# A hybrid RWKV-7 and attention layer: the RWKV batch stage for both token halves in one call, with V centred as it is turned

## The chip, the cores and the metric

The kernel runs on one core of a Trainium2 chip. The metric is the device time of one execution in microseconds; for each kernel the median of several runs is given, and one further execution is profiled. TensorE, VectorE, ScalarE and GpSimd are called PE, DVE, ACT and POOL in the rows, and SP is the engine that issues most DMAs; PEld are weight loads of TensorE.

## What is computed

One decoder layer on 1024 tokens of width 1024, all in float32: a norm and one wide projection; two parallel branches, RWKV-7 time mixing and dilated attention, each behind a sigmoid gate; a cross-attention to 256 memory rows; a squared-ReLU MLP; a last norm. The change lies in the RWKV branch, 16 heads of 64 channels:

```
for each token t and head:               # r, w, k, v, a, b have 64 channels
    sa    = state @ a_t                  # a = -kk, b = kk * a
    state = state * w_t + sa (x) b_t + v_t (x) k_t
    y_t   = state @ r_t
mean, var of y_t over the 64 channels
yn    = (y - mean) * rsqrt(var + eps) * gn_w + gn_b
out   = (yn + sum(r * k * r_k) * v) * g
```

v enters y linearly, channel by channel. So a v whose mean over the 64 channels of its head is taken off gives a y whose mean is zero; the bonus term sum(r k r_k) v needs v as it is.

## The kernel before

**Data.** Tokens are cut in two halves of 512, a half in 8 chunks of 64. Channels lie on the 128 partitions, two heads of 64 at a time: a pair p, eight pairs in all. The recurrence is computed in chunks: all that doesn't depend on the state is done for 8 chunks of a half as a batch of small matrix products, and then `scan` walks the chunks in order with one 64x64 state per head.

**Dense products.** `product` (L138) multiplies an 8 x 128 deep weight with a half of the activations. Weights and activations are split in a high and a low fp32r part, so each of the 8 steps is three matmuls of 128x128 by 512 columns (L143 to L145), and the generator yields after each three. `dense` (L328) does both halves; `proj` makes r, k and v of a pair with it, `gate` the gates.

**Stages of a pair.** `prep_a` makes decay and normed kk from two low-rank products; `psw` and `psa` get one 128-row matmul each with the high part of w2 and a2 and one 64-row matmul with the low part (L452 ff.). `prep_b` makes the tiles a, r, b, k and the products of them (`pa`, L528 ff.): per half two blocks of 8 fp32 matmuls of 64 rows, head 0 on the upper and head 1 on the lower half of the array's rows. VectorE masks them into A. `prep_d` turns V (`pvt`, four transposes) and b, k (`pb`), and multiplies the strictly lower part of A with V. `solve` and `solve_pe` invert a unit lower triangle, the first on VectorE, the second with fp32 matmuls on 32-row and 64-row tiles. `post` has per half a transpose and six batch products with the inverse: it makes the S tile, from which `scan` works. `gnorm` norms the result: `block_sum` sums over a head's 64 channels with a block-diagonal matrix of ones, once for the mean (`pm`) and once for the squares (`pvv`).

**Rows and columns of the array.** A batch product is `both` (L444):

```
ps = pms.tile([P, 8, CH], F32, tag="m", name=nm("po"))
for c in range(8):
    for h, hh in enumerate(heads()):
        mm(ps[hh, c, :], *fn(c, h, hh))
```

The head chooses the output partitions, so the column half of the array; `rows(half)` chooses the input partitions, so the row half. Half 0 works on rows 0 to 63 and half 1 on rows 64 to 127. An fp32 matmul is two instructions in the trace, so one call of `both` is 32. In two of the products (BK with UV, UV with A) all 128 rows are read.

**The order of the work.** `weave` (L151) merges generators: each has a number of steps and a stretch of a nominal 0 to 100, and the step that is due first goes next. The dictionary W (L761) has the due stretches: scan `s0`, `s1`; norm `g0`, `g1`; `b0` to `d1`, `so`, `sp`, `po`, `a0`, `a1` for the preparation of the next pair. `proj` of the pair after that and the gates fill in between. One call of `weave` is one iteration; there are nine, p = -1 to 7, the last without preparation. On top of this order the compiler's planner issues an instruction earlier when it expects that the one ahead isn't ready; `tc.issue_after` holds it to an order.

**PSUM.** Eight banks: two for dense products (`pacc`), three for all small products (`pms`), two for the scan's pz (`psc`), one for its y (`py`).

Of the kernel before, what the change touches and what calls it, by code (L numbers as in the profile page):

```python
# [17 lines left out]
P = 128  # L18
# [23 lines left out]
def hybrid_layer(ctx, tc, x, mem, norm_mix_g, w_in, shift_mu, w0, w2, a0, a2, g2, k_k, k_a, r_k, gn_w, gn_b,  # L42
# [230 lines left out]
    with tc.tile_pool(name="ra", bufs=1, side="right", reuse_waits="tile") as ra, \  # L273
# [3 lines left out]
            tc.tile_pool(name="pms", bufs=3, space=PSUM, reuse_waits="tile") as pms, \  # L277
            tc.tile_pool(name="psc", bufs=2, space=PSUM, reuse_waits="tile") as psc, \
# [29 lines left out]
        nc.vector.tensor_tensor(id2[:, 0, :], ident[:, 0:CH], ident[:, CH:P], op=ALU.add)  # L308
        WD = ra.tile([P, S], F32R, name="WD")
# [18 lines left out]
        def dense(src, evac, m=P):  # L328

            w = wload(src, NK, m, nc.gpsimd)  # L330
            for half in range(2):
                yield from product(w, acts(half), lambda ps: evac(half, ps[0:m, :]), m)

        def low_rank(blk):
# [28 lines left out]
            if blk == 0:  # L363
                evac(0, plr[0])
                yield from product(wlr, acts(1), lambda ps: evac(1, ps))
# [33 lines left out]
        def proj(p, cols="rkv"):  # L399
            if p not in st:  # L400
                st[p] = d = {"rkv": [{}, {}]}
                wa = [(rb if i else wrp[-1]).tile([P, 2, P], dt, tag=("wr", "wa1", "wa2")[i], name=nm("wa"), bufs=1 if i else None)
                      for i, dt in enumerate((F32, F32R, F32R))]
# [40 lines left out]
        def both(fn):  # L444

            ps = pms.tile([P, 8, CH], F32, tag="m", name=nm("po"))
            for c in range(8):
                for h, hh in enumerate(heads()):
                    mm(ps[hh, c, :], *fn(c, h, hh))
            return ps  # L450

        def prep_a(p, half):  # L452
# [3 lines left out]
            wah, wal = d["wa"]  # L456
# [5 lines left out]
            mm(psw, wal[0:64, 0, :], WD[0:64, hs], False, True)  # L462
            mm(psa, wal[64:128, 1, :], AD[64:128, hs], False, True)
# [32 lines left out]
        def prep_b(p, half):  # L496
# [24 lines left out]
            for q in range(2):  # L521
# [19 lines left out]
        def prep_d(p, half):  # L541
# [9 lines left out]
            for q in range(4):  # L551
                nc.tensor.transpose(pvt[:, q, :], v[:, q * P:(q + 1) * P], ident)
# [119 lines left out]
        def post(p, half):  # L672


            d = st[p]
            Am = d["Am"]
            ar, UV, BK, gC = [d[half][x] for x in ("ar", "UV", "BK", "gC")]
            m0 = half * 16
            us = rows(half)[0]
            if half == 0:  # L680
                d["S"] = rA.tile([P, 2, 4, 8, CH], F32, tag="A", name=nm("S"))
            St = d["S"][:, half]
            nc.gpsimd.tensor_tensor(St[:, 0], id2.broadcast_to([P, 8, CH]), gC.broadcast_to([P, 8, CH]), op=ALU.mult)

            pt = pms.tile([P, 4, P], F32, tag="m", name=nm("paT"))
            for q in range(4):
                nc.tensor.transpose(pt[:, q, :], d[half]["ara"][:, 0, 2 * q:2 * q + 2, :], ident)
            WT = r3.tile([P, 8, P], F32, tag="bk", name=nm("WT"), bufs=2)
            wtp = WT[us].rearrange("p (q e) f -> p q e f", e=2)
            nc.scalar.copy(wtp[:, :, 0, :], pt[0:64])  # L690
            nc.vector.tensor_copy(wtp[:, :, 1, :], pt[64:128])
            yield
            pu = both(lambda c, h, hh: (Am[us, m0 + 2 * c + h, 0:64], UV[us, c, hh]))
            for hh in heads():
                nc.scalar.copy(UV[us, :, hh], pu[hh])
            yield
            pw = both(lambda c, h, hh: (Am[us, m0 + 2 * c + h, 0:64], WT[us, c, hh]))

            Wm = Am[us, m0:m0 + 16, 0:64].rearrange("p (c h) t -> p c h t", h=2)
            for h, hh in enumerate(heads()):  # L700
                (nc.vector.tensor_copy if h else nc.scalar.copy)(Wm[:, :, h, :], pw[hh])
            yield
            ps = both(lambda c, h, hh: (Am[us, m0 + 2 * c + h, 0:64], BK[us, c, hh]))
            nc.vector.tensor_tensor(St[:, 0], St[:, 0], ps, op=ALU.add)
            yield
            ps = both(lambda c, h, hh: (BK[:, c, hh], UV[:, c, hh]))
            nc.scalar.copy(St[:, 2], ps)
            yield
            ps = both(lambda c, h, hh: (Am[us, m0 + 2 * c + h, 0:64], Am[us, m0 + 2 * c + h, 64:128]))
            nc.vector.tensor_tensor(St[:, 1], ar[:, :, 1, :], ps, op=ALU.add)  # L710
            yield
            ps = both(lambda c, h, hh: (UV[:, c, hh], Am[:, m0 + 2 * c + h, 64:128]))
            nc.scalar.copy(St[:, 3], ps)
            yield
# [21 lines left out]
        def gnorm(p, half):  # L736
# [7 lines left out]
            pm = pms.tile([P, H2], F32, tag="m", name=nm("pm"))  # L744
            block_sum(pm, y)
            yield
            nc.vector.scalar_tensor_tensor(y, pm, -1.0 / 64, y, op0=ALU.mult, op1=ALU.add)
# [14 lines left out]
                 d1=(28, 38), sp=(36, 54), c0=(40, 44), c1=(45, 49), po=(56, 82), a0=(62, 78), a1=(76, 94))  # L762
        W0 = dict(b0=(20, 29), b1=(28, 37), so=(37, 52), d0=(38, 45), d1=(44, 51), sp=(52, 66), c0=(50, 54), c1=(54, 58),
                  po=(68, 90), a0=(68, 82), a1=(80, 96))
# [4 lines left out]
        for p in range(-1, 8):  # L769
# [9 lines left out]
            if p < 6:  # L779
                cut = 42 if p >= 0 else 50  # L780
                sts.append((proj(p + 2, "krv"), 48, cut, 100))
# [4 lines left out]
            sts.append((chain(*DN), 16 * max(n, 1), 0, cut))  # L786
            if p >= 0:
                sts += [(scan(p, 0), 8, *W["s0"]), (scan(p, 1), 8, *W["s1"]),
                        (gnorm(p, 0), 6, *W["g0"]), (gnorm(p, 1), 6, *W["g1"])]
            if p < 7:  # L790
                for h in "01":
                    sts += [(prep_b(p + 1, int(h)), 5, *V["b" + h]), (prep_d(p + 1, int(h)), 4, *V["d" + h]),
                            (prep_c(p + 1, int(h)), 3, *V["c" + h])]
                sts += [(solve(p + 1), 22, *V["so"]), (solve_pe(p + 1), 10, *V["sp"]),
                        (chain(post(p + 1, 0), post(p + 1, 1)), 14, *V["po"])]
# [907 lines left out]
```

## Time and profile before

| | |
|---|---|
| median of 3 runs | 2513.06 us (2507.98 to 2517.85) |
| profiled execution | 2522.45 us |
| its span | 2520.7 us, mean granted TensorE clock 0.974 |
| RWKV stage in it | some 72 to 1020 us |
| busy over the span | TensorE 95%, VectorE 64%, ScalarE 42%, GpSimd 36% |
| matmul instructions | 18613 |

The span runs from the first to the last instruction. A matmul's length in the timeline has a modelled end and overlaps the next one, so what it costs on a busy TensorE is the time from its start to the start of the next.

### The profile page before, as it was taken

To read this page: it belongs to the slowest core of one execution; us is meant where nothing else is said; L and a number is where in the kernel's file an instruction comes from. 1 tells how busy PE (TensorE), PEld (TensorE's weight loads), DVE (VectorE), ACT (ScalarE), POOL (GpSimd) and SP (SyncE) were. 2 spreads that over 40 slices of the span, in tenths; PEclk is the share of its full clock that TensorE was granted. 3 is DMA by queue.
4 is the path that set the end of the run, shared out by engine and by line. 5 is a ranking of instruction groups with operands and counts; after the bars stand their busy time and mean duration, and the time that the engine had idled before them with its cause. 6 is when DMAs were issued, how large, how long until landed. Compare 5 with 4: busy or idle time off the path is not lost. (4 is left out here: it accounts for less than half of the span.)

```text
span 2520.7 us, 46875 instructions
## 1 busy us (share of the span) xinstructions
PE 2400.2 (95%) x18613; PEld 1886.7 (75%) x18613; DVE 1601.1 (64%) x2754; ACT 1060.0 (42%) x2048; POOL 918.0 (36%) x740
## 2 busy tenths in 40 slices
PE   6999999999999999999999999999979999899997
PEld 5787767777777777777767888788758888577775
DVE  6546675666656642224266565445799999887795
ACT  5434645445454443333344345444432222343344
POOL 4321222212222123211135533523665554556654
PEclk9999999999999999999979999999989999999998
DMA  4221111011111112321145554222234445654342
GB/s 168 54 65 28 36 37 33 29 31 36 37 33 32 39 44 82 83 60 43 47 133 161 162 161 144 82 59 84 71 117 152 152 145 163 192 159 122 109 139 75
DMA packets 301618, 226.72 MB, mean 90 GB/s; under 512 B 16229, under 2 KB 252375, under 8 KB 301399
## 3 DMA queue, kind: packets, MB, share of 16 engines
q1 hardware_dynamic: 301111, 223.20, 29.3%
q8 instruction: 146, 2.39, 0.4%
q10 hardware_dynamic: 288, 0.52, 0.1%
q14 instruction: 73, 0.60, 0.1%
HBM read 169.99 MB, written 53.67 MB: 89 GB/s over the span
## 5 line engine op out<-in xcount | busy, mean ns | idle before, releaser
L143 PE MATMUL acc<-ah,wh 128*128 128x512 f32 (+1 forms) x1600 | 666.7, 417 | 9.7 <-DVE h L1023 3.0
L112 POOL TENSOR_TENSOR wl<-wr,wh 128x512 fp32r<-128x512 f32 x248 | 333.5, 1347 | 820.7 <-ACT wh L110 798.1
L144 PE MATMUL acc<-al,wh 128*128 128x512 f32 (+1 forms) x1600 | 620.5, 388 | 2.8 <-POOL al L231 1.5
L145 PE MATMUL acc<-ah,wl 128*128 128x512 f32 (+1 forms) x1600 | 620.5, 388 | 0.0
L143 PEld LDWEIGHTS acc<-ah,wh 128*128 128x128 f32 x1600 | 303.5, 190 | 83.0 <-issue 7.0
L145 PEld LDWEIGHTS acc<-ah,wl 128*128 128x128 f32 x1600 | 302.8, 189 | 62.1
L144 PEld LDWEIGHTS acc<-al,wh 128*128 128x128 f32 x1600 | 305.2, 191 | 46.3 <-POOL al L231 3.3
L1394 PE MATMUL ms<-ah,wh 128*128 128x512 f32 x768 | 310.2, 404 | 17.2 <-DVE sg L1404 15.7
L1395 PE MATMUL ms<-al,wh 128*128 128x512 f32 x768 | 309.4, 403 | 17.2 <-DVE al L129 12.0
L1396 PE MATMUL ms<-ah,wl 128*128 128x512 f32 x768 | 307.5, 401 | 1.0 <-POOL wl L1357 1.0
L110 ACT CAST wh<-wr 128x512 fp32r<-128x512 f32 (+1 forms) x296 | 179.5, 607 | 289.4 <-PE acc L144 196.9
L1357 POOL TENSOR_TENSOR wl<-ws,wh 128x512 fp32r<-128x512 f32 x128 | 184.2, 1443 | 155.0 <-ACT wh L1356 148.6
L1395 PEld LDWEIGHTS ms<-al,wh 128*128 128x128 f32 x768 | 148.2, 193 | 56.1 <-DVE al L129 17.1
L1394 PEld LDWEIGHTS ms<-ah,wh 128*128 128x128 f32 x768 | 148.1, 193 | 54.7 <-ACT ah L128 8.4
L1357 POOL TENSOR_TENSOR wl<-sr,wh 128x512 fp32r<-128x512 f32 x96 | 142.8, 1488 | 122.2 <-ACT wh L1356 117.4
L1396 PEld LDWEIGHTS ms<-ah,wl 128*128 128x128 f32 x768 | 148.1, 193 | 35.4 <-POOL wl L1357 2.6
L1356 ACT CAST wh<-ws 128x512 fp32r<-128x512 f32 x128 | 79.3, 620 | 203.1 <-PE ms L1395 159.6
L1356 ACT CAST wh<-sr 128x512 fp32r<-128x512 f32 x96 | 59.2, 620 | 137.9 <-PE ms L1395 124.4
L912 DVE CUSTOM_DVE_ANT_0 sS<-pS,bias 128x128 f32<-128x128 f32 (+1 forms) x96 | 30.2, 349 | 114.8 <-PE pS L125 114.4
L129 DVE TENSOR_TENSOR al<-ur,ah 128x512 fp32r<-128x512 f32 x96 | 96.6, 1043 | 0.9 <-ACT ah L128 0.7
L128 ACT CAST ah<-ur 128x512 fp32r<-128x512 f32 x96 | 58.4, 619 | 64.0 <-DMA ur<-uscr 58.4
L917 ACT ACTIVATE sS<-sS,nm 128x128 f32<-128x128 f32 (+1 forms) x96 | 42.5, 443 | 76.6 <-DVE nm L915 72.1
(415 smaller groups left out, 4140.0 us busy)
## 6 DMA issues: line engine op xcount, KB each, us to landing
sr<-in_ffn_w_dram SPq DMA_DIRECT2D x134, 256.0 KB
wr<-in_w_in_dram SPq DMA_DIRECT2D x120, 256.0 KB
ur<-uscr SPq DMA_DIRECT2D x112, 256.0 KB
uscr<-sg SPq DMA_DIRECT2D x93, 256.0 KB
gtscr<-gt SPq DMA_DIRECT2D x32, 256.0 KB
g<-gtscr SPq DMA_DIRECT2D x32, 256.0 KB
wr<-in_p_rwkv_dram SPq DMA_DIRECT2D x32, 256.0 KB
wr<-in_w_out_dram SPq DMA_DIRECT2D x32, 256.0 KB
```

The lines of the kernel that those rows point to most:

```text
L110: nc.scalar.copy(h, raw)
L112: lo_eng.tensor_tensor(l, raw, h.bitcast(F32), op=ALU.subtract)
L128: nc.scalar.copy(hi, src)
L129: (lo_eng or nc.vector).tensor_tensor(lo, src, hi.bitcast(F32), op=ALU.subtract)
L143: mms.append(nc.tensor.matmul(ps, h, ah, start=(k == 0), stop=False))
L144: mms.append(nc.tensor.matmul(ps, h, al, start=False, stop=False))
L145: mms.append(nc.tensor.matmul(ps, l, ah, start=False, stop=(k == len(acts) - 1)))
L1356: nc.scalar.copy(h, raw)
L1357: nc.gpsimd.tensor_tensor(l, raw, h.bitcast(F32), op=ALU.subtract)
L1394: nc.tensor.matmul(ps, h[:, k, :], ah, start=(k == 0), stop=False)
L1395: nc.tensor.matmul(ps, h[:, k, :], al, start=False, stop=False)
L1396: nc.tensor.matmul(ps, l[:, k, :], ah, start=False, stop=(k == 3))
```

## The change

It does six things. (1) `four` takes the place of `both`: it computes the products of both halves in one call, alternating half 0 and half 1 for each chunk, with one PSUM tile for each half; `post` is one generator of 7 steps for both halves, and the batch product at the end of `prep_d` becomes a stage of its own, `prep_e`, due at 37 to 39. In `post` the product of BK and UV now stands ahead of that of A and BK. (2) V is turned by a product with `cen` (the identity less 1/64 within each head's block) and not by a transpose, so that it is centred; `gnorm` loses the sum `pm` and what used it. (3) The `pa` matmuls are chained one behind another by `issue_after`. (4) `product` has a step: in the RWKV stage it yields after six matmuls and not after three, and the numbers of steps are halved. (5) The low parts of w2 and a2 lie in a tile that is zero elsewhere, so that all four matmuls of `prep_a` use 128 rows. (6) `pms` has four banks, `psc` one.

```diff
-    def product(w, acts, evac, m=P, n=H2):
+    def product(w, acts, evac, m=P, n=H2, step=1):
...
-            if k < len(acts) - 1:
+            if k < len(acts) - 1 and k % step == step - 1:
                 yield
...
-            tc.tile_pool(name="pms", bufs=3, space=PSUM, reuse_waits="tile") as pms, \
-            tc.tile_pool(name="psc", bufs=2, space=PSUM, reuse_waits="tile") as psc, \
+            tc.tile_pool(name="pms", bufs=4, space=PSUM, reuse_waits="tile") as pms, \
+            tc.tile_pool(name="psc", bufs=1, space=PSUM, reuse_waits="tile") as psc, \
...
+        wal = ra.tile([P, 2, P], F32R, name="wal")
+        nc.gpsimd.memset(wal.bitcast(F32), 0.0)
+
+        cen = ra.tile([P, P], F32, name="cen")
+        nc.vector.scalar_tensor_tensor(cen, bones_r.bitcast(F32), -1.0 / 64, ident, op0=ALU.mult, op1=ALU.add)
...
-                yield from product(w, acts(half), lambda ps: evac(half, ps[0:m, :]), m)
+                yield from product(w, acts(half), lambda ps: evac(half, ps[0:m, :]), m, step=2)
...
-                nc.gpsimd.tensor_tensor(wa[2], wa[0], wa[1].bitcast(F32), op=ALU.subtract)
-                d["wa"] = wa[1:]
+                for j in range(2):
+                    js = slice(64 * j, 64 * j + 64)
+                    nc.gpsimd.tensor_tensor(wal[js, j, :], wa[0][js, j, :], wa[1][js, j, :].bitcast(F32), op=ALU.subtract)
+                d["wa"] = wa[1]
...
+        def four(fn):
+
+
+            ps = [pms.tile([P, 8, CH], F32, tag="m", name=nm("po")) for _ in range(2)]
             for c in range(8):
-                for h, hh in enumerate(heads()):
-                    mm(ps[hh, c, :], *fn(c, h, hh))
+                for half in range(2):
+                    for h, hh in enumerate(heads()):
+                        mm(ps[half][hh, c, :], *fn(half, c, h, hh))
             return ps
...
-            mm(psw, wal[0:64, 0, :], WD[0:64, hs], False, True)
-            mm(psa, wal[64:128, 1, :], AD[64:128, hs], False, True)
+            mm(psw, wal[:, 0, :], WD[:, hs], False, True)
+            mm(psa, wal[:, 1, :], AD[:, hs], False, True)
...
-                first = pa(0, 1)
-                with tc.issue_after(first.ins):
-                    pa(0, 0)
-                    for i in range(1, 4):
-                        for h in range(2):
-                            pa(i, h)
+                last = pa(0, 1)
+                for i in range(4):
+                    for h in range(2 if i else 1):
+                        with tc.issue_after(last.ins):
+                            last = pa(i, h)
...
-                nc.tensor.transpose(pvt[:, q, :], v[:, q * P:(q + 1) * P], ident)
+
+                mm(pvt[:, q, :], v[:, q * P:(q + 1) * P], cen)
...
-            ps = both(lambda c, h, hh: (d["Am"][vs, half * 16 + 2 * c + h, 0:64], UV[vs, c, hh]))
-            for hh in heads():
-                nc.scalar.copy(UV[us, :, hh], ps[hh])
+
+        def prep_e(p):
+            d = st[p]
+            UV = [d[half]["UV"] for half in range(2)]
+            ps = four(lambda half, c, h, hh: (d["Am"][rows(half)[1], half * 16 + 2 * c + h, 0:64],
+                                              UV[half][rows(half)[1], c, hh]))
+            for half in range(2):
+                for hh in heads():
+                    nc.scalar.copy(UV[half][rows(half)[0], :, hh], ps[half][hh])
             yield
...
-        def post(p, half):
+        def post(p):
...
+            pu = four(lambda f, c, h, hh: (am(f, c, h), UV[f][us(f), c, hh]))
+            for f in range(2):
+                for hh in heads():
+                    nc.scalar.copy(UV[f][us(f), :, hh], pu[f][hh])
+            yield
+            pw = four(lambda f, c, h, hh: (am(f, c, h), WT[f][us(f), c, hh]))
...
+            ps = four(lambda f, c, h, hh: (BK[f][:, c, hh], UV[f][:, c, hh]))
+            for f in range(2):
+                nc.scalar.copy(St[:, f, 2], ps[f])
+            yield
+            ps = four(lambda f, c, h, hh: (am(f, c, h), BK[f][us(f), c, hh]))
...
-            pm = pms.tile([P, H2], F32, tag="m", name=nm("pm"))
-            block_sum(pm, y)
-            yield
-            nc.vector.scalar_tensor_tensor(y, pm, -1.0 / 64, y, op0=ALU.mult, op1=ALU.add)
             nc.scalar.activation(q, y, AF.Square)
...
-                (chain(post(p + 1, 0), post(p + 1, 1)), 14, *V["po"])]
+                (prep_e(p + 1), 1, *V["e"]), (post(p + 1), 7, *V["po"])]
```

## Rows read from the trace of the kernel before

**Rows 1.** The page: engine shares (busy us, share of the span, instructions).

```profile
PE 2400.2 (95%) x18613; PEld 1886.7 (75%) x18613; DVE 1601.1 (64%) x2754; ACT 1060.0 (42%) x2048; POOL 918.0 (36%) x740
```

**Rows 2.** Sums by stretch, six pair iterations (TensorE, loads, VectorE, ScalarE, GpSimd; clock, DMA).

```profile
230.00:860.00 630.00, 609.36 (x8413) 462.16 (x8415) 416.15 (x827) 312.59 (x473) 129.08 (x120) 0.98 0.12 33
```

**Rows 3.** Sums by stretch, one iteration in five parts.

```profile
541.70:576.00 34.30, 33.14 (x332) 23.58 (x334) 28.67 (x73) 14.06 (x23) 4.80 (x4) 1.00 0.11 31
576.00:588.00 12.00, 10.17 (x295) 8.20 (x297) 5.32 (x9) 2.08 (x4) 5.28 (x7) 0.72 0.21 68
...
600.00:636.30 36.30, 35.66 (x474) 26.98 (x473) 22.36 (x36) 25.89 (x39) 7.56 (x7) 1.00 0.11 31
...
sum 105.60, PE 101.97 PEld 77.41 DVE 69.10 ACT 52.11 POOL 21.55; mean PE 20.39 PEld 15.48 DVE 13.82 ACT 10.42 POOL 4.31
```

**Rows 4.** Timeline of TensorE, dense products and batch blocks (start us, length us).

```profile
602.61 0.40 PE L144 MATMUL acc<-al,wh 128*128 128x512 f32 x1
602.84 0.40 PE L145 MATMUL acc<-ah,wl 128*128 128x512 f32 x1
603.17 1.15 PE L125 MATMUL po<-UV,A 64*64 64x64 f32 x32
604.25 0.50 PE L143 MATMUL acc<-ah,wh 128*128 128x512 f32 x1
...
605.14 1.15 PE L125 MATMUL po<-WT,A 64*64 64x64 f32 x32
```

**Rows 5.** Timeline of TensorE, the solve's blocks on four tiles.

```profile
575.96 1.99 PE L125 MATMUL ps<-A,DD 32*32 32x64 f32 x128 [0.42 <-DVE DD L617]
...
580.70 1.87 PE L125 MATMUL ps<-DD,A 32*64 32x32 f32 x77 [1.83 <-issue]
...
590.81 2.07 PE L125 MATMUL ps<-DD,KX 32*64 32x32 f32 x128
```

**Rows 6.** Timeline of TensorE, the pa blocks.

```profile
544.63 3.10 PE L125 MATMUL pa<-ar,bk 64*128 64x128 f32 x32
...
550.21 1.16 PE L125 MATMUL pa<-ar,bk 64*128 64x128 f32 x16
...
552.57 0.49 PE L125 MATMUL pa<-ar,bk 64*128 64x128 f32 x2
...
554.48 0.50 PE L143 MATMUL acc<-ah,wh 128*128 128x512 f32 x1
```

**Rows 7.** Timeline of TensorE, A with BK and prep_a's products.

```profile
625.44 0.33 PE L125 MATMUL po<-BK,A 64*64 64x64 f32 x2
...
627.38 0.51 PE L143 MATMUL acc<-ah,wh 128*128 128x512 f32 x1
...
628.19 0.40 PE L125 MATMUL psw<-WD,wa 128*128 128x512 f32 x1
...
629.33 0.86 PE L125 MATMUL po<-UV,BK 128*64 128x64 f32 x22
```

**Rows 8.** Groups of instructions: TensorE 230 to 860 us, VectorE 541.7 to 576 us.

```profile
L125 PE MATMUL pm<-sp,bones_r 128*128 128x512 f32 x12 | 5.4, 447 | 0.0
...
L747 DVE SCALAR_TENSOR_TENSOR y<-pm,y 128x512 f32<-128x512 f32 x1 | 0.7, 690 | 0.9 <-PE pm L125 0.9
L434 DVE TENSOR_TENSOR sl<-y,sp 128x512 fp32r<-128x512 f32 x1 | 0.7, 685 | 0.0
```

**Rows 9.** Timeline of TensorE, transposes of V and fp32 products of the norm.

```profile
557.04 0.66 PE L552 MATMUL pvt<-ident,v 128*128 128x128 f32 x4
...
1481.29 1.06 PE L125 MATMUL ms<-rs,ones 128*128 128x128 f32 x8
```

**Rows 10.** Timeline of all engines, one scan step.

```profile
555.38 0.33 PE L125 MATMUL pz<-Z,S 64*64 64x64 f32 x4
...
555.75 0.50 PE L143 MATMUL acc<-ah,wh 128*128 128x512 f32 x1
555.80 0.21 DVE L731 TENSOR_TENSOR Z<-pz,S 128x64 f32<-128x64 f32 x1
```

More of the change, by code (lines that the diff above doesn't have):

```diff
@@ L364, in low_rank @@
                 evac(0, plr[0])
-                yield from product(wlr, acts(1), lambda ps: evac(1, ps))
+                yield from product(wlr, acts(1), lambda ps: evac(1, ps), step=2)
             elif blk == 1:
@@ L670, in solve_pe, with us, am @@
                 yield
-        def post(p, half):
+        def post(p):
             d = st[p]
             Am = d["Am"]
[L677 to L691, printed above, removed]
+            ar, UV, BK, gC = [[d[half][x] for half in range(2)] for x in ("ar", "UV", "BK", "gC")]
+            d["S"] = rA.tile([P, 2, 4, 8, CH], F32, tag="A", name=nm("S"))
+            St = d["S"]
+            for f in range(2):
+                nc.gpsimd.tensor_tensor(St[:, f, 0], id2.broadcast_to([P, 8, CH]), gC[f].broadcast_to([P, 8, CH]),
+                                        op=ALU.mult)
+            def us(f):
+                return rows(f)[0]
+            def am(f, c, h):
+                return Am[us(f), 16 * f + 2 * c + h, 0:64]
+            WT = []
+            for f in range(2):
+                pt = pms.tile([P, 4, P], F32, tag="m", name=nm("paT"))
+                for q in range(4):
+                    nc.tensor.transpose(pt[:, q, :], d[f]["ara"][:, 0, 2 * q:2 * q + 2, :], ident)
+                WT.append(r3.tile([P, 8, P], F32, tag="bk", name=nm("WT"), bufs=2))
+                wtp = WT[f][us(f)].rearrange("p (q e) f -> p q e f", e=2)
+                nc.scalar.copy(wtp[:, :, 0, :], pt[0:64])
+                nc.vector.tensor_copy(wtp[:, :, 1, :], pt[64:128])
@@ L692, in post @@
             yield
-            pu = both(lambda c, h, hh: (Am[us, m0 + 2 * c + h, 0:64], UV[us, c, hh]))
-            for hh in heads():
-                nc.scalar.copy(UV[us, :, hh], pu[hh])
+            pu = four(lambda f, c, h, hh: (am(f, c, h), UV[f][us(f), c, hh]))
+            for f in range(2):
+                for hh in heads():
+                    nc.scalar.copy(UV[f][us(f), :, hh], pu[f][hh])
             yield
-            pw = both(lambda c, h, hh: (Am[us, m0 + 2 * c + h, 0:64], WT[us, c, hh]))
@@ L702, in post @@
             yield
-            ps = both(lambda c, h, hh: (Am[us, m0 + 2 * c + h, 0:64], BK[us, c, hh]))
-            nc.vector.tensor_tensor(St[:, 0], St[:, 0], ps, op=ALU.add)
+            ps = four(lambda f, c, h, hh: (BK[f][:, c, hh], UV[f][:, c, hh]))
+            for f in range(2):
+                nc.scalar.copy(St[:, f, 2], ps[f])
             yield
-            ps = both(lambda c, h, hh: (BK[:, c, hh], UV[:, c, hh]))
-            nc.scalar.copy(St[:, 2], ps)
+            ps = four(lambda f, c, h, hh: (am(f, c, h), BK[f][us(f), c, hh]))
@@ L708, in post @@
+            for f in range(2):
+                nc.vector.tensor_tensor(St[:, f, 0], St[:, f, 0], ps[f], op=ALU.add)
             yield
-            ps = both(lambda c, h, hh: (Am[us, m0 + 2 * c + h, 0:64], Am[us, m0 + 2 * c + h, 64:128]))
-            nc.vector.tensor_tensor(St[:, 1], ar[:, :, 1, :], ps, op=ALU.add)
+            ps = four(lambda f, c, h, hh: (am(f, c, h), Am[us(f), 16 * f + 2 * c + h, 64:128]))
+            for f in range(2):
+                nc.vector.tensor_tensor(St[:, f, 1], ar[f][:, :, 1, :], ps[f], op=ALU.add)
@@ L711, in post @@
             yield
-            ps = both(lambda c, h, hh: (UV[:, c, hh], Am[:, m0 + 2 * c + h, 64:128]))
-            nc.scalar.copy(St[:, 3], ps)
+            ps = four(lambda f, c, h, hh: (UV[f][:, c, hh], Am[:, 16 * f + 2 * c + h, 64:128]))
+            for f in range(2):
+                nc.scalar.copy(St[:, f, 3], ps[f])
             yield
```

27 lines of the change are left out of this document (13 added, 14 removed).

## The prediction

> **What bounds the kernel now.** I read the page's engine shares first: TensorE is busy 95% of the span, VectorE 64% [rows 1]. The change touches the RWKV stage only, so next come the sums by stretch: from 230 to 860 us, six pair iterations of some 105 us, TensorE is busy 609 of 630 us [rows 2]. It is the bound there, and what an instruction costs is its slot, the time to the start of the next one. Inside one iteration (541.7 to 647.3 us) the sums by stretch show who comes second: VectorE 28.67 of 34.3 us in the scan stretch, ScalarE 25.89 of 36.3 in the post stretch, and a granted clock of 0.72 from 576 to 588 us, so about half of those 12 us at 1.2 instead of 2.4 GHz [rows 3]. Then the timeline of TensorE, for slots. A dense matmul takes 0.23 us (602.61 to 602.84); a batch block of one half, 32 instructions, 1.08 us (603.17 to 604.25); three dense matmuls between two blocks 0.89 us (604.25 to 605.14), not 0.69. So an island of small matmuls costs 0.20 us beside its own time [rows 4].
>
> **The batch blocks.** An iteration has 14 (two in prep_d, twelve in post). Ten read 64 rows of the array, a group that is fixed by the half; four read all 128 (UV with BK, A with UV). Two halves in one call are four tiles at once, each half with its own PSUM bank. Would four run abreast? The nearest rows say yes: the solve's 128 instructions on four 32-row tiles take 1.99 us, 16 ns each against 34 in a batch block, and those of four 32-row groups by 64 columns, where two groups share the columns and write different banks, are as fast (2.07 us) [rows 5]. Bounds: 64 instructions at 16 ns, 1.00 us, and at 34 ns, 2.16 us. I take 1.08, the time of one half: the solve's tiles stream up to as many columns per instruction. Removed: 5 x 1.08 = 5.40 us. The Trainium skill (TensorE: Matmul & The Clock Gate, "Wait — 56ns, not 53.3ns?") speaks against this: it says that starts never come closer than about 25 ns. By that rule a four would take an estimated 1.6 us, and the five would bring 2.8 us. The 16 ns of these rows disagree.
>
> The two 128-row calls keep their work: nothing, or 0.15 us each for one entry and exit less; I take 0.3 in all. Seven islands fewer: 7 x 0.20 = 1.40 us. prep_e copies its result out with four ScalarE instructions, as before, in a stretch where ScalarE is busy 2.08 of 12 us [rows 3]. A four holds two of the four banks of pms until it is copied out, and the next call gets the other two, so TensorE waits only if ScalarE falls a whole call behind (rival 1).
>
> **The order in post.** A with BK needs the inverse that ScalarE and VectorE have just copied, and waits: 1.94 us (625.44 to 627.38) instead of 1.08 [rows 7]. In the new order the UV product stands ahead of it and covers this copy; gain 0.86 at most here and less in the other half, nothing at least. I take 1.1 for both.
>
> **pa in pairs.** A good block of 16 lasts 1.16 us. The planner orders by its own estimate of what is ready, and two of four blocks lose their pairing: the block of 32 lasts 3.10 us against twice 1.16, and from 552.57 to the next dense product at 554.48 it is 1.91 us, with a wait for VectorE's masking in it [rows 6]. A chain restores the pairing, and the fourth bank of pms lets the next two tiles start while the last two are masked: 0.78 + 0.75 = 1.53 us; at least half of it, if the wait stays.
>
> **V centred.** Four block-sum matmuls go: between 4 x 0.23 (a dense slot) and 4 x 0.45 (the row's mean); 1.3 us. A cast on ScalarE and two VectorE instructions of 0.69 us a half go with them, off the path [rows 8]. The four transposes of V become true fp32 products of eight instructions: 0.66 us now, 1.06 for the same shape in the norm, so +0.40 twice, +0.8 us [rows 9].
>
> **Smaller edits.** prep_a's two 64-row products become 128-row ones: four matmuls from 628.19 to 629.33, 1.14 us, become 4 x 0.23 = 0.92 and no longer an island [rows 7]; -0.5 for both halves. The low parts are two subtractions instead of one on POOL, busy under 8 of 36.3 us there [rows 3]: nothing, and if POOL were full it would be under 1 us. One bank instead of two for the scan's pz costs nothing: the next pz needs the Z that VectorE makes by reading this bank. No DMA is added.
>
> **Sixes.** 64 dense pieces of an iteration become 32. In the scan stretch that can merge up to eight islands, -1.6 us. Against it, a scan step without dense work behind it must wait: pz starts at 555.38, VectorE makes Z from 555.80 to 556.01 [rows 10], so the next could start 0.63 us after it at best, where the step itself fills 0.37 (555.38 to 555.75): 0.26 x 8 = +2.1 us, and more where VectorE's queue is full. I take -0.6.
>
> **Sum.** -5.40 -1.40 -0.30 -1.10 -1.53 -1.30 +0.80 -0.50 -0.60 = -11.3 us an iteration. What is late next: the scan stretch falls to some 28 us of TensorE work, about VectorE's busy time; the post stretch to some 29, with ScalarE at 25.9. Two engines so near each other don't overlap fully; the cost is between nothing and all their present idle time (5.6 and 10.4 us). I take 1.5 us each, +3.0, hence -8.3. Six iterations: -50. The first preparation (before 230 us) has the fours and islands but no scan: -7. The last one -8, the final iteration without preparation -1. Together **-66 us**. The profiled execution took 2522.45 us (span 2520.7); the median of the runs shown is 2513.06, 9.4 less, and the difference is taken off that: **2447 us**.
>
> **Rivals.**
> 1. VectorE and ScalarE become the bound. If they keep all their idle time, the post stretch gains nothing and the scan stretch only 1.4 us (the two VectorE instructions that go there): -1.4 x 6 - 16 = -24, 2489 us. For: 84% and 71% busy in the stretches that shrink. Against: TensorE is idle only 3.6 of these 105.6 us [rows 3], so it is its order that sets most of the idle time of the others. 12%.
> 2. The fours don't run abreast, because the planner parts the halves (as it parted pa, and no chain is laid on the fours) or because tiles are issued no faster than 34 ns: 8 x 5.4 = 43 us are lost, -23, 2490 us. Against: the solve's first block stands unparted, 16 ns apart [rows 5]. 8%. Halfway, by the 25 ns that the Trainium skill states, it would be an estimated -44 us, 2469; I hold that within the 8%.
> 3. More: the engines overlap as now (-18 more), and the clock drop after the solve goes, as prep_e stands between: the granted 0.98 of 630 us is worth 13 us [rows 2]. -97, 2416 us. 10%.
> 4. Slower: instruction supply. With 77 of the 128 instructions of the solve's second block still to come TensorE waits 1.83 us, and the profile names nothing but "issue" [rows 5]. A four issues twice as densely as a block now. If each of the seven brought such a wait: 7 x 1.83 x 8 = 102 us, net +36, 2549 us; from 4.5 waits a pair on, the gain is gone. Against: the wait comes only where 256 small matmuls stand back to back; a four has 64, and dense products between. 5%. The Trainium skill (Runtime: NRT & Kernel Launch, "Instruction fetch mechanics") says that fetching hides behind the issue of instructions; by that this wait would be zero, and the row disagrees.
>
> **Numbers.** My forecast has 65%. The range, 2412 to 2484, holds it, rival 3 nearly whole, and the milder half of 1 and 2; left out are rival 4 and the rest of 1 and 2, some 17%. Half a per cent (12.6 us) is about what a measurement of this kernel tells from no change; all cases but the fourth are faster by more, but for 1% at their weak ends: 94%; of the fourth's 5%, where only some of the calls wait, 1% comes out within it: 2%, and 4% slower.
>
> **What would show it.** Right: batch blocks of 64 instructions in about 1.1 us (64-row) and 2.0 us (128-row), seven a pair; pa blocks of 16 all at 1.16 us; no pm, pvt blocks of 8 in some 0.8 us; iterations of 95 to 99 us; waits for VectorE in the scan and for ScalarE in post slightly longer. Wrong: fours of 2.1 us (rival 2); iterations above 101 us with TensorE idle on VectorE or ScalarE (1); "issue" waits inside the fours (4).

## The result and the profile after

| | before | after |
|---|---|---|
| median | 2513.97 us of 4 runs (2507.98 to 2517.85) | 2441.62 us of 4 runs (2437.65 to 2445.95) |
| ratio, 95% interval | | 0.9707 (0.9688 to 0.9727) |
| profiled execution | 2522.45 us, span 2520.7 | 2439.77 us, span 2438.1 |
| mean granted clock | 0.974 | 0.983 |

The change gains 72 us; 66 were forecast, the time at 2447 us. The two profiled executions lie 82.7 us apart, 10 more than the medians. That part is not in the RWKV stage: from the first product of the attention (`pS`, at 1020.4 us before, at 949.8 after) to the end it is 1500.3 us before and 1488.3 after, and 1491.0 in a second profile of the kernel before.

The page's engine shares answer to [rows 1]. TensorE lost 96 us of busy time, VectorE 12, and their shares are what they were:

```profile
PE 2304.0 (95%) x18645; PEld 1834.2 (75%) x18645; DVE 1589.6 (65%) x2723; ACT 1046.3 (43%) x2032; POOL 922.5 (38%) x749
```

Seen by the starts of the iterations (the first `pz`), the first preparation gained 8.4 us (7 forecast), the six pair iterations 53.4 (50), the last with a preparation 7.0 (8), the final one 1.8 (1): together 70.6. Sums by stretch of one iteration after, in the same five parts as [rows 3] (us, busy time of TensorE, its loads, VectorE, ScalarE and GpSimd, then clock, DMA share, GB/s):

```profile
506.30:542.00 35.70, 31.73 (x285) 23.29 (x284) 32.10 (x75) 13.92 (x22) 7.54 (x8) 1.00 0.17 52
542.00:555.00 13.00, 11.58 (x416) 9.74 (x417) 5.28 (x9) 4.40 (x9) 2.49 (x3) 0.87 0.02 6
555.00:566.00 11.00, 11.00 (x218) 9.15 (x211) 6.09 (x10) 5.05 (x7) 1.79 (x2) 1.00 0.01 3
566.00:593.00 27.00, 26.44 (x459) 21.08 (x458) 19.54 (x31) 19.37 (x32) 6.84 (x6) 1.00 0.15 41
593.00:602.60 9.60, 9.60 (x43) 7.69 (x41) 5.79 (x13) 7.44 (x12) 3.16 (x4) 1.00 0.16 43
sum 96.30, PE 90.34 PEld 70.95 DVE 68.81 ACT 50.17 POOL 21.82; mean PE 18.07 PEld 14.19 DVE 13.76 ACT 10.04 POOL 4.36
```

The post stretch fell from 36.3 to 27.0 us, by 9.3, as much as the whole iteration (105.6 to 96.3). Some of that is work that only moved: the stretch holds 60 dense matmuls and held 68, and the eight transposes `paT` (0.7 us) now stand ahead of it. At a slot of 0.23 us that is 2.6 us, so work for work the post stretch fell by about 6.7. The scan stretch did not shrink at all: 34.3 became 35.7 us, though a batch block of each half and two of the four `pm` matmuls left it. It holds 62 dense matmuls now, and held 51; at a slot of 0.23 us these 11 are 2.5 us, so work for work it fell by about 1.1. VectorE is busy 32.1 of its 35.7 us, and TensorE idle for 4.0.

The slots of the small matmuls, from each start to the next start and summed over the six pair iterations (53.4 us gained), tell where the gain is. The 64-row batch products (`prep_e`'s and three of `post`) took 71.7 us and take 32.7, with their waits. `pm` took 7.9 and is gone, V's turning took 4.9 and takes 10.3. The `pa` blocks took 36.2 us and take 36.2.

The waits of TensorE say for what, over six iterations before (us in total, times, longest us; behind the engine that is waited for stands the tile that it has to write):

```profile
PE ps L125 <- issue: 8.0, 6, 1.8
PE po L125 <- DVE A L701: 3.3, 6, 0.5
PE ps L125 <- DVE DD L617: 2.6, 6, 0.4
PE pz L125 <- DVE Z L731: 2.5, 7, 0.9
PE pa L125 <- DVE A L537: 2.1, 6, 0.3
```

and over six iterations after:

```profile
PE pz L125 <- DVE Z L760: 19.3, 23, 1.3
PE ps L125 <- issue: 6.1, 7, 1.2
PE ps L125 <- DVE DD L633: 4.9, 6, 0.8
PE po L125 <- DVE A L726: 3.4, 6, 0.6
```

The scan's wait for Z, the state that VectorE must make before the next step, rose from 2.5 to 19.3 us. It is what came late next. The wait of `pa` for VectorE's masking is gone, and its four blocks take 4.6 us an iteration where they took 6.0. But right behind the last of them the scan now waits for Z, so nothing is left of that gain:

```profile
517.99 1.16 PE L125 MATMUL pa<-ar,bk 64*128 64x128 f32 x16
520.50 0.33 PE L125 MATMUL pz<-Z,S 64*64 64x64 f32 x4 [1.34 <-DVE Z L760]
```

The wait for VectorE's copy of the inverse (A) is as long as before, in another place.

The batch products, in TensorE's timeline after. First a 64-row call for both halves, 64 instructions, from its start to the next start 1.09 us; the same took [rows 4] 1.08 for one half:

```profile
567.46 1.16 PE L125 MATMUL po<-UV,A 64*64 64x64 f32 x64
568.55 0.50 PE L143 MATMUL acc<-ah,wh 128*128 128x512 f32 x1
...
575.02 0.40 PE L125 MATMUL pss<-sp,bones_r 128*128 128x512 f32 x1
575.58 0.34 PE L125 MATMUL po<-UV,BK 128*64 128x64 f32 x4
576.48 1.97 PE L125 MATMUL po<-UV,BK 128*64 128x64 f32 x60 [0.56 <-DVE A L726]
578.38 0.50 PE L143 MATMUL acc<-ah,wh 128*128 128x512 f32 x1
...
589.01 2.09 PE L125 MATMUL po<-A,UV 128*64 128x64 f32 x64
591.02 0.50 PE L143 MATMUL acc<-ah,wh 128*128 128x512 f32 x1
```

All 64-row calls of these iterations read like the first. The 128-row ones keep their work: 2.01 us for the last row here. UV with BK, which now stands ahead of A with BK, stops after four instructions, where its second half begins, until VectorE has copied A out, and lasts 2.80. It doesn't read A; what it needs is the bank. Between the two calls `prep_a` takes a bank for its sum `pss`, so the second half of UV with BK gets one that the call just before it has filled. In the last preparation, which has no `prep_a` beside it, the call lasts 2.02. A with BK no longer waits and lasts 1.09 where [rows 7] had 1.94.

### The profile page after: what moved, and what is told of

Same layout as the page of the kernel before. It is cut to its first block, busy times and chain, and to the rows that moved or that the text cites. A ratio compares the mean times of both kernels' runs of the same rounds, so it can differ in the third digit from the quotient of the medians.

```text
span 2438.1 us, 46897 instructions
## 1 busy us (share of the span) xinstructions
PE 2304.0 (95%) x18645; PEld 1834.2 (75%) x18645; DVE 1589.6 (65%) x2723; ACT 1046.3 (43%) x2032; POOL 922.5 (38%) x749
## 3 DMA queue, kind: packets, MB, share of 16 engines
q1 hardware_dynamic: 301111, 223.20, 30.2%
## 5 line engine op out<-in xcount | busy, mean ns | idle before, releaser
L143 PE MATMUL acc<-ah,wh 128*128 128x512 f32 (+1 forms) x1600 | 652.2, 408 | 11.3 <-DVE h L1048 3.0
L1420 PE MATMUL ms<-al,wh 128*128 128x512 f32 x768 | 308.6, 402 | 15.6 <-DVE al L129 10.3
L937 DVE CUSTOM_DVE_ANT_0 sS<-pS,bias 128x128 f32<-128x128 f32 (+1 forms) x96 | 30.2, 349 | 114.6 <-PE pS L125 114.4
```

What stands on the lines that cost most here:

```text
L1420: nc.tensor.matmul(ps, h[:, k, :], al, start=False, stop=False)
```

## Experiments

Each kernel is the kernel after with the edit shown, and was run beside the kernel before on one chip. Ratios are to that, with their 95% intervals; differences are to the 2441.62 us of the kernel after. The kernel before took 2512.1 to 2516.0 us on these chips, and the work behind the RWKV stage, which no edit touches, takes 1485.8 to 1495.8 us in the profiles of these kernels. So where a difference is small, the end of the RWKV stage in the profile is given too (949.8 us in the kernel after).

**Post by halves.** Is the gain of post its merging, or is that hidden?

```diff
-            pu = four(lambda f, c, h, hh: (am(f, c, h), UV[f][us(f), c, hh]))
...
+            pu = both(lambda c, h, hh: (Am[us, m0 + 2 * c + h, 0:64], UV[us, c, hh]))
...
-                        (prep_e(p + 1), 1, *V["e"]), (post(p + 1), 7, *V["po"])]
+                        (prep_e(p + 1), 1, *V["e"]), (chain(post(p + 1, 0), post(p + 1, 1)), 14, *V["po"])]
```

> The changed kernel with post half by half again, in its old order of products, 14 steps (prep_e, banks, sixes, V and pa as changed). Theory now, after halves kept apart cost only 9 us (the abreast tiles save slots, but VectorE, ScalarE and the instruction supply take most of it back): the merged post is worth its slots 4 x 1.08 + 0.3 and six islands 1.2 us a pair, 47 us in all, of which about half shows: +18 to +30 us, 2460 to 2472. The prediction's sum without any cover: +47 us or more, 2488. Rival (post's merging is worth no more than its abreast tiles): +9 us, 2451.

2495.91 us, 0.9923 (0.9909 to 0.9937): 54 us of the 72 are gone, about what the prediction's terms for post come to without any cover (55, worked out below), and not the 18 to 30 of the theory. The edit gives back the old order of the products too. Each block of a half takes 1.08 us, iterations last some 102.5, and the waits for A are 8.0 us on VectorE and 1.7 on ScalarE, where the kernel after has 3.4:

```profile
PE po L125 <- DVE A L725: 8.0, 12, 1.1
...
PE po L125 <- ACT A L725: 1.7, 6, 0.3
```

**Halves apart inside the call.** This leaves the merged stages, the banks and the number of islands, and takes away only that neighbouring instructions work on different rows.

```diff
-            for c in range(8):
-                for half in range(2):
+            for half in range(2):
+                for c in range(8):
```

> The changed kernel, but a four does all of half 0 and then all of half 1 (same 64 instructions, same banks, same merging of blocks). Theory (four tiles abreast carry the gain): the five 64-row calls take 2.0 us instead of 1.09, +0.93 x 5 x 8 pairs = +37 us on 2441.6, so 2479; the two 128-row calls stay at 2.01. Rival (the gain comes from the merged calls, the sixes and the clock, not from abreast tiles, or VectorE and ScalarE bound post as well): below +12 us, 2441 to 2454.

2450.41 us, 0.9751 (0.9724 to 0.9778): only 8.8 us lost (the stage ends at 957.5), as the rival had it. The slots did move, from 1.09 to 1.84 us in the timeline (1.84 is less than twice 1.08):

```profile
569.29 1.91 PE L125 MATMUL po<-UV,A 64*64 64x64 f32 x64
571.13 0.50 PE L143 MATMUL acc<-ah,wh 128*128 128x512 f32 x1
```

Five such calls in eight preparations are 5 x 8 x 0.75 = 30 us of slots. What gave 21 back stands in the waits and in the clock. In the solve, its second block follows the call of `prep_e`. In the kernel after it stops for 1.07 us after 14 instructions, with nothing but "issue" named:

```profile
542.35 1.99 PE L125 MATMUL ps<-A,DD 32*32 32x64 f32 x128 [0.82 <-DVE DD L633]
544.27 1.16 PE L125 MATMUL po<-UV,A 64*64 64x64 f32 x64
545.36 0.43 PE L125 MATMUL ps<-DD,A 32*64 32x32 f32 x14
546.86 1.88 PE L125 MATMUL ps<-DD,A 32*64 32x32 f32 x114 [1.07 <-issue]
```

With the halves apart it doesn't stop here (in three of the six iterations a gap of 0.3 us is left):

```profile
546.05 1.99 PE L125 MATMUL ps<-A,DD 32*32 32x64 f32 x128 [0.82 <-DVE DD L633]
547.97 1.91 PE L125 MATMUL po<-UV,A 64*64 64x64 f32 x64
549.81 2.26 PE L125 MATMUL ps<-DD,A 32*64 32x32 f32 x128
```

Over six iterations the 6.1 us of issue waits are gone. So are the 3.4 us of waiting for A (UV with BK lasts 2.02 us), and the wait for Z is 16.8 instead of 19.3 us. The clock records show no time at 1.2 GHz in the RWKV stage, and 10.2 us in the kernel after; half of that, some 5 us, is what it can have cost. That is up to 6.1 + 3.4 + 2.5 + 5 = 17 of the 21 us.

What stands behind "issue" can be read in the DMA records. In the profiles of all kernels here this block of the solve has 75 stops of over 0.5 us, and each of them ends 1.2 to 1.6 us after a transfer of 16 KB on the instruction queue q8 has landed; of moments taken at random, 4 in 100 lie so. The page of the kernel after has 147 such transfers:

```profile
q8 instruction: 147, 2.41, 0.4%
```

That is one for some 254 of TensorE's matmuls and weight loads (18645 of each), so for some 127 matmuls. At 15 to 17 ns a matmul it makes one transfer every 2 us, and a transfer alone takes 0.9 to 1.6. So the stop reads as TensorE waiting for its instructions, though no run changed the fetching itself.

**Three banks.** The small products get back their three banks.

```diff
-            tc.tile_pool(name="pms", bufs=4, space=PSUM, reuse_waits="tile") as pms, \
-            tc.tile_pool(name="psc", bufs=1, space=PSUM, reuse_waits="tile") as psc, \
+            tc.tile_pool(name="pms", bufs=3, space=PSUM, reuse_waits="tile") as pms, \
+            tc.tile_pool(name="psc", bufs=2, space=PSUM, reuse_waits="tile") as psc, \
```

> The changed kernel with three banks for small products and two for pz, as before. Theory (the fourth bank lets the next call start while the last is copied out, and it, not the chain, restored the pairing of pa): calls of post wait for their copies, up to 0.8 us in three to five of seven calls a pair, and pa's second blocks wait again: +15 to +35 us, 2457 to 2477. Rival (dense work between the calls covers the copies): below +5 us.

2478.77 us, 0.9856 (0.9840 to 0.9871): 37 us lost, half of the whole gain and a little more than the theory had. The timeline shows both of its effects. A `pa` block breaks after 2 instructions and goes on 1.78 us later, as [rows 6] do; and a call of both halves, which takes two banks at once, gets the second one late:

```profile
533.21 0.49 PE L125 MATMUL pa<-ar,bk 64*128 64x128 f32 x2
...
534.99 1.16 PE L125 MATMUL pa<-ar,bk 64*128 64x128 f32 x14 [0.63 <-DVE A L546]
...
585.85 0.56 PE L125 MATMUL po<-UV,A 64*64 64x64 f32 x10
587.50 1.15 PE L125 MATMUL po<-UV,A 64*64 64x64 f32 x54 [1.09 <-DVE WT L714]
588.58 0.50 PE L143 MATMUL acc<-ah,wh 128*128 128x512 f32 x1
```

That call lasts 2.73 us and not 1.09. The waits of six iterations name the bank's readers one by one, none of which stands in the list of the kernel after:

```profile
PE po L125 <- DVE WT L714: 6.5, 6, 1.1
...
PE po L125 <- DVE S L734: 4.1, 6, 0.7
PE pa L125 <- DVE A L546: 3.8, 6, 0.6
```

By slots over six iterations the loss isn't in `pa`: with the waits right behind its blocks it takes 30.2 us here and 36.2 with four banks. The batch calls take 14 us more, the solve's second block 7.6 more. Up to 7 us of the 37 are the clock, 23.9 us at 1.2 GHz in the stage instead of 10.2.

**pa unchained.** Four banks, but the planner may order the matmuls of the blocks behind the first one as it likes.

```diff
-                last = pa(0, 1)
-                for i in range(4):
-                    for h in range(2 if i else 1):
-                        with tc.issue_after(last.ins):
-                            last = pa(i, h)
+                first = pa(0, 1)
+                with tc.issue_after(first.ins):
+                    pa(0, 0)
+                    for i in range(1, 4):
+                        for h in range(2):
+                            pa(i, h)
```

> The changed kernel with the pa matmuls held only behind the first one, as before. Sum of the prediction: the chain was worth 1.5 us a pair, so +11 us, 2452. Theory now (pa's blocks stand in the stretch that VectorE bounds, and a wait for masking or for Z remains): +2 to +7 us, 2444 to 2449. Rival (the fourth bank alone restored the pairing, as the waits that broke it are gone): 0, and all pa blocks at 1.09 us.

2440.89 us, 0.9709 (0.9679 to 0.9738): nothing, and every block keeps the time that it has with the chain. Two of them in the timeline, each with 1.09 us to the next start:

```profile
510.94 1.16 PE L125 MATMUL pa<-ar,bk 64*128 64x128 f32 x16
512.03 0.33 PE L125 MATMUL pz<-Z,S 64*64 64x64 f32 x4
...
514.38 1.16 PE L125 MATMUL pa<-ar,bk 64*128 64x128 f32 x16
515.47 0.33 PE L125 MATMUL pz<-Z,S 64*64 64x64 f32 x4
```

So the pairs come from the fourth bank, not from the chain: with three banks the chain stood and the block broke, with four it is gone and none does.

**V turned without centring.** The transpose and the block sum for the mean come back.

```diff
-                mm(pvt[:, q, :], v[:, q * P:(q + 1) * P], cen)
+                nc.tensor.transpose(pvt[:, q, :], v[:, q * P:(q + 1) * P], ident)
...
+            pm = pms.tile([P, H2], F32, tag="m", name=nm("pm"))
+            block_sum(pm, y)
+            yield
+            nc.vector.scalar_tensor_tensor(y, pm, -1.0 / 64, y, op0=ALU.mult, op1=ALU.add)
```

> The changed kernel with V transposed again and the mean taken off in the norm (pm and its cast and two VectorE instructions are back). By TensorE's slots alone: +1.0 us of pm less 0.9 us of V's products, about 0 a pair, so 2441 +- 4. Theory (the scan stretch is bound by VectorE, 32.1 of 35.7 us busy): +1.4 us a pair of VectorE work in the scan stretch shows in the time, +8 to +14 us, 2450 to 2456. Rival (VectorE is busy there but off the path): within 4 us of 2441.6.

2450.90 us, 0.9745 (0.9718 to 0.9772): 9.3 us lost, twice the 0.5 x 8 = 4 us that the prediction had for the TensorE slots; the stage ends at 955.6, 5.8 later. The theory's time came, but its reason is not shown: the waits for Z are shorter here, and those for VectorE's DD and A longer (six iterations).

```profile
PE pz L125 <- DVE Z L760: 13.6, 12, 1.3
PE ps L125 <- DVE DD L633: 8.2, 6, 1.4
...
PE po L125 <- DVE A L726: 4.9, 6, 0.8
```

With 1.4 us for WT that makes 28.1 us of waiting for VectorE, and 27.6 in the kernel after. The slots of `pm` come to 6.2 us in these iterations and V's turning saves 4.7, so 2 us in eight preparations and not 4. What makes up the rest stays open.

**Threes.** Dense work is again asked for three matmuls at a time.

```diff
-                yield from product(w, acts(half), lambda ps: evac(half, ps[0:m, :]), m, step=2)
+                yield from product(w, acts(half), lambda ps: evac(half, ps[0:m, :]), m)
...
-                sts.append((proj(p + 2, "krv"), 24, cut, 100))
+                sts.append((proj(p + 2, "krv"), 48, cut, 100))
...
-            sts.append((chain(*DN), 8 * max(n, 1), 0, cut))
+            sts.append((chain(*DN), 16 * max(n, 1), 0, cut))
```

> The changed kernel with dense pieces of three matmuls again. Theory (sixes were worth little: fewer islands against scan steps that wait for VectorE): between -3 and +8 us, so 2438 to 2450; waits of pz for VectorE's Z fall from 19.3 us (six iterations) to under 8, and islands come back. Rival A (the sixes carry a good part of the gain): +15 us or more. Rival B (they cost more by the waits than they save): -8 us or more.

2443.41 us, 0.9714 (0.9687 to 0.9742): no difference that these intervals can tell. The waits for Z fall to 11.8 us in six iterations (not under 8), and 6.3 us of dense products that wait for VectorE's `carry` come in their place.

**prep_e late, and the kernel before once more.** Does the place of `prep_e`, between two blocks of the solve, set the clock there?

```diff
-                 d1=(28, 38), sp=(36, 54), c0=(40, 44), c1=(45, 49), e=(37, 39), po=(56, 82), a0=(62, 78), a1=(76, 94))
+                 d1=(28, 38), sp=(36, 54), c0=(40, 44), c1=(45, 49), e=(53, 55), po=(56, 82), a0=(62, 78), a1=(76, 94))
```

> The changed kernel with prep_e due at 53 to 55 (after the solve's matmuls) and not at 37 to 39, where it came to stand between the solve's first two blocks; the same work otherwise. Theory (its place between these blocks is worth something by itself: it spreads the dense instruction traffic, so the issue wait in the second block shrinks and the granted clock falls more seldom): the issue wait is back at 1.8 us an iteration (6 us in all now, 8 or more then), half clock in the RWKV stage goes from 10 us back to 20 to 30 us, and the time rises by 5 to 14 us, 2447 to 2455. Rival (the clock fell less by chance, the place does nothing): 2441 +- 4 and half clock of 10 us or less.

> The kernel before, unchanged, for a second profile. Question: is the granted clock lost in the solve, 30.6 us at half clock between 60 and 1000 us in the first profile (10.2 us in that of the changed kernel, 0 to 24 in its variants), a property of that kernel or of one execution? Theory (a property of its order: the solve's two first blocks stand back to back and one waits 1.8 us for issue): 24 to 37 us again, and issue waits of 7 to 9 us. Rival (chance): under 14 us.

2447.35 us, 0.9733 (0.9714 to 0.9752), so 5.7 us lost (the intervals overlap; the stage ends at 956.4, 6.6 later): issue waits of 7.7 us and new waits for WT (2.9 and 1.4 us, in `psw` and `psa`). Time at 1.2 GHz in the RWKV stage, from the clock records: 6.8 us with `prep_e` late, 10.2 in the kernel after, and 30.7 in both profiles of the kernel before (2514.59 us in the second). It fell in five of the six iterations, in both. So it is a trait of the kernel before and not of one execution; and the theory fails by which the place of `prep_e` had ended it. With three banks it is 23.9 us, in the other variants 0 to 20.5, with one profile of each.

**VectorE relieved.** If VectorE holds the scan, work taken off it must bring time. Its scaling of `bk` goes to GpSimd and one copy to ScalarE:

```diff
-            nc.vector.tensor_tensor(bk, bk, gC.unsqueeze(3).broadcast_to([P, 8, 2, CH]), op=ALU.mult)
+            nc.gpsimd.tensor_tensor(bk, bk, gC.unsqueeze(3).broadcast_to([P, 8, 2, CH]), op=ALU.mult)
...
-            nc.vector.tensor_copy(uvp[vs, :, 1, :], pvt[64:128])
+            nc.scalar.copy(uvp[vs, :, 1, :], pvt[64:128])
```

> The changed kernel with two kinds of VectorE instructions of the scan stretch moved: the scaling of b and k by gC to GpSimd, the second half of V's copy to ScalarE (2 x 1.23 + 2 x 0.69 = 3.8 us of 32.1 a pair leave VectorE). Theory (the scan stretch is bound by VectorE): 1.5 to 3 us a pair of six to seven, 10 to 20 us faster, 2421 to 2432; waits of pz for Z fall from 19.3 us to under 12. Rival (VectorE is busy there but the wait is the chain PE, VectorE, PE itself): within 4 us of 2441.6; GpSimd's longer instruction may even make it slower.

2434.14 us, 0.9676 (0.9658 to 0.9695): 7.5 us gained (the stage ends at 935.3, 14.5 earlier), less than the theory's 10 and more than the rival's 4. The waits for Z fall to 11.4 us. In the stretch below VectorE is busy 28.55 of 33.7 us, where the kernel after has 32.1 of 35.7; the two aren't the same work, as this one already holds 226 small matmuls of the solve and of `prep_e`, and 48 dense matmuls instead of 62:

```profile
498.30:532.00 33.70, 31.43 (x491) 24.34 (x490) 28.55 (x73) 15.16 (x25) 11.12 (x9) 1.00 0.15 48
```

Then two further edits on top of this one, each alone. One puts a second gate's dense work into each of the six iterations, to fill the waits, and takes it from the ends:

```diff
-        GD = [4, 1, 1, 1, 1, 1, 1, 4, 2]
+        GD = [0, 2, 2, 2, 2, 2, 2, 3, 1]
```

> The VectorE relief (b and k scaled on GpSimd, the second half of V's copy on ScalarE), and the sixteen gate products dealt out 0, 2, 2, 2, 2, 2, 2, 3, 1 over the nine iterations instead of 4, 1, 1, 1, 1, 1, 1, 4, 2: the dense work is the same, but six more gates stand in scan stretches. Theory (these stretches wait for VectorE, 12.3 us for Z in six iterations with the relief alone, and dense work there fills the wait): iterations grow by less than the 11.0 us of a gate, the first shrinks by 44, and the sum gains 4 to 12 us on 2434, 2422 to 2430. Rival (the dense work only lengthens the stretch, as the planner had already drawn dense pieces forward): 2434 +- 4, or slower where the last preparation lacks a gate.

The other takes one more product off VectorE:

```diff
-            nc.vector.tensor_tensor(ar[:, :, 1, :], c3(r), c3(G), op=ALU.mult)
+            nc.gpsimd.tensor_tensor(ar[:, :, 1, :], c3(r), c3(G), op=ALU.mult)
```

> The VectorE relief, and r times G (0.69 us twice a pair, in the scan stretch) on GpSimd too. Theory (VectorE still bounds the stretch, 28.6 of 33.7 us busy): another 0.5 to 1.2 us a pair, 4 to 9 us on 2434, 2425 to 2430. Rival (GpSimd's instruction of some 1.3 us comes late for pa, and the stretch is now held by the chain itself): 2434 +- 3 or slower.

With the gates 2422.43 us, 0.9636 (0.9619 to 0.9653); with the product 2423.08 us, 0.9640 (0.9621 to 0.9660): 11 to 12 us more each. With the gates each of the six iterations, with 11.0 us more of dense work, grew by 7.9 us, so 19 of 66 us cost nothing. Ten of them are waits for Z, which are all but gone:

```profile
PE pz L125 <- DVE Z L760: 1.4, 5, 0.5
```

With the product the waits for Z stay what they were, 10.9 us after 11.4, so its 11 us, more than the theory had, aren't that wait. Issue waits fall by 1.7 us, and the time at 1.2 GHz from 13.7 to 3.4 us, worth up to 5; the rest is open.

Both together:

> The VectorE relief with r times G on GpSimd and the gate products dealt out evenly, together. Theory (both work on the same wait, pz for Z, which is 12 us with either relief alone and 2.3 us once the gates are spread): the gains overlap, 2 to 8 us on 2422, 2414 to 2420. Rival (they add up, as less VectorE work shortens the stretch also where nothing waits): 11 us, 2411. Rival (nothing is left in it): 2422 +- 3.

2416.68 us, 0.9606 (0.9588 to 0.9624). That is 5.8 us on top of the gates and not 11, but the two intervals overlap, and in the profiles the stage ends no earlier (929.7, and 927.7 with the gates alone). So it isn't shown that the product adds anything to the gates. This version has the lowest median of all.

## Why the prediction was right

**The fours run abreast: as forecast.** 1.09 us against 1.08, all 64-row calls alike, and rival 2 falls. A rule of the Trainium skill (TensorE: Matmul & The Clock Gate, "Wait — 56ns, not 53.3ns?") has starts never closer than about 25 ns; 1.09 us for 64 instructions is 17 ns, so the measurement disagrees with it here too. But this step had priced the abreast rows at 5.40 us an iteration as if the slots were the time. Taken away alone, they cost 8.8 us in all, a fifth of 43: TensorE then waits less elsewhere. The merging of post as a whole, with its islands and the order, is worth 54 us. Its terms in the sum, 4 x 1.08 + 6 x 0.20 + 0.30 + 1.10 = 6.9 an iteration, are 55 us over eight preparations without any cap. The parts don't add up, and only the step as a whole was sized right.

**The caps: the sum right, the parts wrong.** 1.5 us an iteration were put on VectorE in the scan and 1.5 on ScalarE in post. ScalarE held nothing: it is busy 19.4 of 27.0 us, and none of the larger waits of TensorE names it. VectorE cost about twice what was taken, 19.3 us of waiting for Z in six iterations, 3.2 each (0.4 before). So half of rival 1 came true: the scan stretch gained about 1.1 us, work for work. The first relief kernel and the one with the gates show this cause, as the waits for Z fall with the time; the 25 us of all edits together (2441.6 to 2416.7) are not all of this kind.

**The order in post: 0.86 us of the 1.1 came, and went.** A with BK no longer waits. The wait for VectorE's copy of A moved one call ahead, to UV with BK (0.56 us, and 2.80 us for the call instead of 2.0). This is the step that failed plainly: it had named ScalarE's and VectorE's copies as covered, and that of four banks the next call gets the other two. But `prep_a`'s sum takes one in between, and the call that was to cover the copies needs a bank that they free.

**The fourth bank: mis-sized.** It stood in the sum through `pa` alone, 1.53 us an iteration or 12 us, and with the chain for a cause. It is worth 37 us, up to 7 of them by the clock, and the chain nothing. The term itself, for `pa`, brought nothing that is left: the blocks take 1.4 us less an iteration, and `pz` waits 1.34 us behind the last. That calls of two banks each wait for their readers when there are three was stated, but not priced.

**V centred and the sixes.** The centring brings 9 us instead of 4 by the medians, and 6 in the stage of the profile; whether VectorE's saved instructions make the difference isn't shown. The sixes were put at a gain of 0.6 us an iteration, some 5 in all, though the prediction's own two bounds, -1.6 and +2.1, add up to a loss; they bring nothing that can be measured. The low parts (0.5) read much as forecast, four `psw` and `psa` matmuls in 0.92 us. They weren't tried alone.

**Instruction supply: rival 4 wrong in place.** No call of both halves waits for "issue" in the kernel after. (With the gates dealt out evenly `prep_e`'s does in two iterations, 1.6 us.) The solve's second block still does: 6.1 us in six iterations, 8.0 before. The kernel with halves apart ends it by slowing one call of 64 instructions by 0.75 us, and the instruction transfers that land before each stop bear out the rival's cause. The Trainium skill (Runtime: NRT & Kernel Launch, "Instruction fetch mechanics") lets fetching hide behind issue; the rows disagree in every iteration of the kernel before.

**The clock: the part of rival 3 that came.** Time at 1.2 GHz in the stage fell from 30.7 to 10.2 us, up to 10 us gained that the forecast's sum did not hold. One iteration before, and the slowest after:

```profile
436.60:541.70 105.10, 101.75 (x1397) 77.28 (x1396) 69.09 (x138) 52.18 (x80) 21.56 (x21) 0.97 0.12 33
```

```profile
602.60:699.10 96.50, 90.46 (x1401) 71.28 (x1400) 68.84 (x134) 50.21 (x78) 21.82 (x21) 0.98 0.12 36
```

Three of five such iterations after stand at 1.00. Rival 3's reason, the place of `prep_e`, is not borne out by the kernel with `prep_e` late. Which edit made the clock fall less stays open.

So 66 against 72 us is right in the main mechanism, the merged calls, whose slots fell as forecast. That the sum came so near is in part luck, since the errors offset: the bank and the clock brought more, VectorE in the scan took more, `pa`, the sixes and the order in post brought nothing.

## What to carry to other kernels

A saved slot on the busiest engine is worth its time only as far as nothing else comes late there: look at the waits around the place, and try the part alone before a gain is credited to it. When calls become larger, count the buffers that they hold at once, and price what happens with one fewer. After the bound has been relieved, shift the second engine's work out of the stretch where it is now late, or bring work into it that needs only the engine that waits; here the two together gave another 25 us. When an engine issues many small instructions at once, look at its instruction transfers too.

## What the runs showed of the hardware

Small fp32 matmuls on four different tiles start 15 to 17 ns apart, whether they are 32-row or 64-row tiles, and two tiles of 64 rows 34 ns apart. When a block of half 0 is followed by one of half 1 without dense work between, the two take 1.84 us and not 2.16.

At that rate TensorE stops for 1.0 to 2.0 us (start to start) without a named releaser, once in the solve of each of the six pair iterations before and after, and goes on 1.2 to 1.6 us after a 16 KB transfer of instructions has landed. How many matmuls run before it isn't fixed: counted from the start of the solve's first block it is 157, 164, 172, 179, 187, 194 in the six iterations before, and 196 to 213 after. It moves by the same step from one iteration to the next, as a border in the instruction stream would. With one call stretched by 0.75 us, at most 0.35 us of the stop is left.

The granted clock fell to half in the solve, behind a stop of this kind, in five of six iterations of the kernel before; it did not fall where the stop was gone (halves apart), but some stops stayed without a fall (post by halves: 6.0 us of issue waits in six iterations, and 3.4 us at half clock in the whole stage). Whether one brings the other was not tried.
